# Layer 0 of a two-layer trunk: a new order of the input products, the gates' products ahead of their sigmoids, and one sum of the attention behind a split

## The chip, the cores and the metric

The kernel runs on one core of one Trainium2 chip, in one launch. The metric is device time in microseconds (us), the median of several executions. The engines by the names of the profile: PE multiplies matrices (PEld loads its weights), DVE is VectorE, ACT is ScalarE, POOL is GpSimd, SP issues most DMAs.

## The reference

A trunk of two layers over 256 positions of width 2048, in float32. Layer 0 projects the normed input into six parts of 1024 columns, runs two recurrences on them side by side, and multiplies their joined outputs by `w_out`. Layer 1 is a dilated windowed attention. Each layer ends in a squared-ReLU MLP. The part that the change is about, cut:

```python
def rg_lru(xb, w_a, b_a, w_i, b_i, lam):          # xb: conv of the x part, 4 blocks of 256
    r = sigmoid(xh @ w_a + b_a); i = sigmoid(xh @ w_i + b_i)      # block by block
    log_a = -LRU_C * r * softplus(-lam)
    a = exp(log_a)
    u = sqrt(-expm1(2.0 * log_a)) * (i * xf)
    return associative_scan(lambda l, r: (l[0] * r[0], r[0] * l[1] + r[1]), (a, u), axis=1)[1]

def recurrent_mixers(h, ...):
    x_lru, y_lru, q_h, f_h, v_h, g_h = split(h @ w_in)
    lru = rg_lru(causal_depthwise_conv(x_lru, conv_w, conv_b), ...) * gelu(y_lru)
    hg = hgrn2(q_h, f_h, v_h, g_h, lower_bound, g_norm)   # per head: normed, times silu(g_h)
    return concatenate([lru, hg], axis=-1) @ w_out
```

## The kernel before

**Products.** Every float32 operand is split into a rounded high part and the rest: `hi` is a cast on ACT (L130), `lo` is weight minus `hi` on DVE (L131). A product is three passes on PE: high by high, high by low, low by high (`mm`, L221). The weights come as blocks of 128x2048 in a fixed list of units; `fetch` loads the next block into one of three `raw` buffers and casts it, two units ahead of the one in use. `hi` has three buffers, so the cast of a block waits for the last product that reads the block three units earlier. Activations are split in the same way by `split_to`: a copy on ACT (L267, or L270 with a gain) and a subtraction on DVE (L268, or L271).

**Layer 0's input products.** `tokens_group` computes 512 columns of the projection in four units of 24 products, into two banks `p` of PSUM (three buffers), and ACT copies them out as a tile `tk` (L369). The names are those of the string ORDER: x and y are the input and the gelu branch of the RG-LRU (two groups each), q, f, v and g belong to HGRN2 (two groups each), and G0 and G1 are the block-diagonal gates of the two RG-LRU groups (`lru_gates`): four banks each, alternately `p` and `pl`, and in each bank two products of 256 columns, each with its sigmoid (L252, priority by `urgent`), followed by the gates' tail on ACT and DVE (L623 to L632), which ends in a scan.

**Ticks.** Everything else of layer 0 is cut into generators, in lanes: a and b hold HGRN2's chunks (`hgrn`), c the convolution (`lru_in`), the gelu (`lru_gelu`) and the RG-LRU's output (`lru_out`), d HGRN2's norm and output gate (`finish`). Each group of products has a list in TICKS of up to eight entries; after every twelve products the next entry advances the lanes that it names. `turned` transposes four 128x128 blocks on PE (L224) into a bank with one buffer each: `po` for `lru_in`, `lru_out` and `finish`; `pd` and `pt` for `hgrn`. Whoever writes such a bank waits until its last reader is done.

**Order on each engine.** A scheduler fixes the order of the instructions on every engine when the kernel is built, by its own costs and priorities; at run time each engine takes its queue strictly in that order, as the rows of the trace show. `after(...)` adds a tie that says which of two instructions of one engine comes first.

**Output product and attention.** `out_project` multiplies the two halves of the mixers' output (`bufb`, 16 blocks of 128 columns: the first eight from the RG-LRU, the other eight from HGRN2) by `w_out`, in the order of its last argument. The large products of both layers use sums of weight blocks: `combine` loads blocks, adds them on DVE (L159) or by an accumulating DMA of POOL (L174), and splits the sums like any block.

Of the kernel before, what the change touches and what calls it, by code (L numbers as in the profile page):

```python
# [10 lines left out]
F32 = mybir.dt.float32  # L11
# [4 lines left out]
AF = mybir.ActivationFunctionType  # L16
OP = mybir.AluOpType
# [3 lines left out]
P = 128  # L21
S = 256
# [19 lines left out]
def trunk_kernel(ctx, tc, head, x, xtok, cols, tab, masks, pos, fin, w_in, w_gate, w_out, w_qkv, w_o, w1, w2, out):  # L42
# [3 lines left out]
    act = pool("act")  # L46
# [5 lines left out]
    pmm = pool("pmm", 3, space=PSUM)  # L52
    psc = pool("psc", 1, space=PSUM)

    stream = lambda: tc.high_priority(offset=PRIO)
    urgent = lambda: tc.high_priority(offset=URGENT)
    V, A, T = nc.vector, nc.scalar, nc.tensor
# [18 lines left out]
    bufb = Chunks()  # L76
# [7 lines left out]
    units = []  # L84
    made = {}
# [11 lines left out]
    for g, step in enumerate(ORDER.split()):  # L97
        if step[0] == "G":
            units.append((w_gate, int(step[1])))
        else:  # L100
            units.extend((w_in, 4 * PLACE[step] + i) for i in range(4))
    units.extend((w_out, 4 * n + g) for n in range(2) for g in (0, 2, 1, 3))
    plan2(w_out, 8)
    for layer in range(2):
        if layer:
# [47 lines left out]
    def combine(u, src, i, what, i0):  # L153
        def load(name, j, home=wraw):
            held[name] = home.tile([P, 2048], F32, name="raw" if home is wraw else name)
            nc.sync.dma_start(held[name], src[j])

        def add(to, x, y):
            return V.tensor_tensor(held[to], held[x], held[y], OP.add)  # L159

        if what == "a":
            load("t1", i0 + 4, both)
            load("a", i)
            held["s"] = both.tile([P, 2048], F32, name="s")
            add("s", "a", "t1")
        elif what in ("n", "d"):
            load(what, i)
        def make(step=2048):
            made[u] = Weights(held[{"t1": "s", "t2": "s", "t3": "t1", "t4": "s"}.get(what, what)], step)

        ahead = units[u + 1][2:3] if u + 1 < len(units) else ()
        if ahead == ("t2",):
            load("c", i0 + 5)
            nc.gpsimd.dma_start(held["t1"], src[i0 + 5], accum_op=OP.add)  # L174
            if (src is w2 and i0 == LATE_SUM) or (src is w1 and i0 == 64):
                make()
                after(add("s", "s", "c"), [made[u].ins.name])
                return
            add("s", "s", "c")
        make(2048 if what != "t2" else 0)  # L180
        if what == "t2":
            waiting.append(made[u])
        if what == "c":
            nc.gpsimd.dma_start(held["s"], src[i0 + 1], accum_op=OP.add)
# [66 lines left out]
    def lut(out_, in_, func, **kw):  # L251
        i = A.activation(out_, in_, func, **kw)  # L252
        if luts["kind"] != tables[func]:
            luts.update(kind=tables[func], before=luts["now"], now=[])
        luts["now"].append(after(i, luts["now"][:1] or luts["before"]))

    def direct(p, w, jobs):
        for blk, mov, first, last in jobs:
            h, l = w.part(blk * P, P)
            mm(p, h, mov[:, :S], start=first, stop=False)  # L260
            mm(p, h, mov[:, S:], start=False, stop=False)
            mm(p, l, mov[:, :S], start=False, stop=last)
# [114 lines left out]
    m = tmp.tile([P, 2], F32, name="nm2", bufs=2)  # L377
# [91 lines left out]

    rotary()  # L470
    done = {"v0": vfirst}
    outs, roots = {}, {}

    def turned(name, tiles, at):
        p = psc.tile([P, 2, S], F32, name=name, bufs=1)
        for i, (z, m) in enumerate(zip(tiles, at)):
            for j in range(2):
                turn(p[:, i, j * P:j * P + P], z[:, j, m * P:m * P + P])
        return p
# [90 lines left out]
    def finish(g, half):  # L570
        if not half:
            hs = roots[g]
            V.tensor_scalar(hs, hs, 1.0 / P, EPS, op0=OP.mult, op1=OP.add)
            roots[g] = wk.tile([P, 8], F32, name="hr", bufs=2)
            rsqrt(roots[g], hs, 8)
        pair_ = [2 * half, 2 * half + 1]
        for at in pair_:
            o, z = outs[4 * g + at], done[f"g{g}"][:, :, at * P:at * P + P]
            s = wk.tile([P, 2, P], F32, name="g", bufs=2)
            lut(s, z, AF.Sigmoid)  # L580
            V.tensor_tensor(s, s, z, OP.mult)
            for j in range(2):
                V.scalar_tensor_tensor(o[:, j], o[:, j], roots[g][:, 2 * at + j:2 * at + j + 1], s[:, j],
                                       op0=OP.mult, op1=OP.mult)
        yield
        p = turned("po", [outs[4 * g + at] for at in pair_], (0, 0))
        if g and not half:
            bufb.tiles[3] = act.tile([P, 4, 2 * S], F32R, name="bufb3")
        for i, at in enumerate(pair_):
            split_to(bufb[:, 8 + 4 * g + at], p[:, i], col("gn", 4 * g + at))  # L590
        yield
# [15 lines left out]

    def lru_gates(gp):
        w = unit(w_gate, gp)
        room = act.tile([P, 8, S], F32, name="bufb3")  # L610
        gr, gi = room[:, :4], room[:, 4:]
        for m in range(4):
            b = 4 * gp + m
            both_p = psc.tile([P, 512], F32, name="pl", bufs=2) if m % 2 else pmm.tile([P, 512], F32, name="p")
            for gate, (g, bname) in enumerate(((gr, "b_a"), (gi, "b_i"))):
                p = both_p[:, gate * S:gate * S + S]
                direct(p, w, [(gate * 8 + 2 * m + k, bufb[:, (b // 2) * 2 + k], k == 0, k == 1)
                              for k in range(2)])
                with urgent():
                    lut(g[:, m], p, AF.Sigmoid, bias=col(bname, b))  # L620
        for m in range(4):
            b = 4 * gp + m
            V.tensor_tensor(xc[:, b], xc[:, b], gi[:, m], OP.mult)  # L623
            lut(gi[:, m], gr[:, m], AF.Tanh, scale=sp4[:, b:b + 1])
            lut(gr[:, m], gr[:, m], AF.Exp, scale=sp8[:, b:b + 1])
            V.tensor_scalar(gi[:, m], gi[:, m], -1.0, 1e-30, op0=OP.mult, op1=OP.max)
        for m in range(4):
            b = 4 * gp + m
            lut(gi[:, m], gi[:, m], AF.Sqrt)
            V.scalar_tensor_tensor(gi[:, m], gr[:, m], 1.0, gi[:, m], op0=OP.add, op1=OP.mult)  # L630
            V.tensor_tensor(xc[:, b], xc[:, b], gi[:, m], OP.mult)
            V.tensor_tensor_scan(xc[:, b], gr[:, m], xc[:, b], 0.0, op0=OP.mult, op1=OP.add)  # L632

    def lru_gelu(n):
        y = done[f"y{n}"]
        q = outs[f"y{n}"] = vgs.tile([P, 2, 512], F32, name="tk", bufs=7)
        for j in range(2):
            A.activation(q[:, j], y[:, j], AF.Square, scale=math.sqrt(0.044715))
            V.scalar_tensor_tensor(q[:, j], q[:, j], 1.0, y[:, j], op0=OP.add, op1=OP.mult)
            lut(q[:, j], q[:, j], AF.Sigmoid, scale=2.0 * math.sqrt(2.0 / math.pi))  # L640
            V.tensor_tensor(y[:, j], y[:, j], q[:, j], OP.mult)
            yield

    def lru_out(n, half):
        b0 = 4 * n + 2 * half
        p = turned("po", [done[f"y{n}"]] * 2, (2 * half, 2 * half + 1))
        z = outs[f"y{n}"][:, half].rearrange("p (i s) -> p i s", i=2)
        V.tensor_tensor(z, p, xc[:, b0:b0 + 2], OP.mult)
        split_to(bufb[:, b0:b0 + 2], z)
        yield  # L650

    def reload():
        for j in range(2):
# [2 lines left out]
    lanes.update(a=[hgrn(0), hgrn(2)], b=[hgrn(1), hgrn(3)],  # L656
                 c=[lru_in(0, 0), lru_in(0, 1), lru_in(1, 0), lru_in(1, 1),
                    lru_gelu(0), lru_out(0, 0), lru_out(0, 1), lru_gelu(1), lru_out(1, 0), lru_out(1, 1)],
                 d=[finish(0, 0), finish(0, 1), finish(1, 0), finish(1, 1)])
    for step in ORDER.split()[1:]:  # L660
        if step == "g1":
            reload()
        if step[0] == "G":
            lru_gates(int(step[1]))
        else:
            done[step] = tokens_group(step, rt)
# [8 lines left out]
    def close_mixers():  # L675
# [3 lines left out]
        formx = both.tile([P, 4, 2, 512], F32R, name="formx")  # L679
        pair, formh = open_pairs(0)  # L680

    ticks[:] = TICKS["o0"].split()
    steps[:] = [[], [], [close_mixers]]

# [253 lines left out]
                second(layer * 64 + q * 16, n, ends, r2, r2n, done, gains if ends and not gname and not n else None)  # L938
        return fing

    nrm = out_project(w_out, "nmlp0", (0, 2, 1, 3))
    nx1 = Norm()
    mlp(0, nrm, nx1, "nmix1")
    pairs.close()
# [192 lines left out]
LATE_SUM = 56  # L1137
PRIO = 150
URGENT = 400
ORDER = "v0 q0 f0 x0 q1 f1 v1 x1 G0 g0 y0 G1 y1 g1"  # L1140
TICKS = {
# [11 lines left out]
}  # L1153
PLACE = {step: n for n, step in enumerate(step for step in ORDER.split() if step[0] != "G")}
WARM = 9
# [101 lines left out]
```

## Time and profile before

| | us |
|---|---|
| median of 3 runs | 2153.93 |
| lowest and highest | 2153.9, 2154.84 |
| profiled execution | 2153.29 |
| span in its trace | 2151.5 |
| PE busy | 2127.6 (99%) |
| DVE busy | 1781.4 (83%) |
| ACT busy | 1307.3 (61%) |

The mean granted clock of PE is 0.996. Layer 0's input products lie in the first 330 us of the span, the attention's first products around 1130 us. Rows of the timeline name start, duration, engine, line, operation, written tile, read tiles and shape; what stands in brackets is the idle time of that engine just before, and what ended it. Matmuls are pipelined, and the modelled end of one lies beyond the start of the next.

### The profile page before, as it was taken

To read this page: it belongs to the slowest core of one execution; us is meant where nothing else is said; L and a number is where in the kernel's file an instruction comes from. 1 tells how busy PE (TensorE), PEld (TensorE's weight loads), DVE (VectorE), ACT (ScalarE), POOL (GpSimd) and SP (SyncE) were. 2 spreads that over 40 slices of the span, in tenths; PEclk is the share of its full clock that TensorE was granted. 3 is DMA by queue.
4 is the path that set the end of the run, shared out by engine and by line. 5 is a ranking of instruction groups with operands and counts; after the bars stand their busy time and mean duration, and the time that the engine had idled before them with its cause. 6 is when DMAs were issued, how large, how long until landed. Compare 5 with 4: busy or idle time off the path is not lost.

```text
span 2151.5 us, 24903 instructions
## 1 busy us (share of the span) xinstructions
PE 2127.6 (99%) x9854; PEld 1770.5 (82%) x9854; DVE 1781.4 (83%) x1687; ACT 1307.3 (61%) x1305; POOL 72.3 (3%) x89
## 2 busy tenths in 40 slices
PE   9999889999999999999999999999999999999998
PEld 7888778888888888888887888888888888888887
DVE  7666567988888889889897888698987988888897
ACT  7443665666557557557665666666655755755764
POOL 0000000000000000000000000000000000000000
PEclk9999899999999999999999999999999999999999
DMA  8444445778887877878687766667778788777885
GB/s 340 161 152 141 153 157 205 229 236 248 273 249 229 280 245 238 256 263 247 222 271 250 237 202 213 217 187 258 236 242 273 247 242 259 267 237 245 267 268 156
DMA packets 70164, 500.12 MB, mean 232 GB/s; under 512 B 7840, under 2 KB 8096, under 8 KB 10272
## 3 DMA queue, kind: packets, MB, share of 16 engines
q1 hardware_dynamic: 57888, 412.99, 50.6%
q0 software_dynamic: 11872, 84.94, 21.1%
q8 instruction: 77, 1.26, 0.2%
q10 hardware_dynamic: 288, 0.61, 0.1%
q14 instruction: 39, 0.32, 0.0%
HBM read 496.41 MB, written 2.10 MB: 232 GB/s over the span
## 4 chain that ended last, share of the span: by engine, by line
PE 95%; ACT 2%; DVE 1%; DMA 1%; issue 0%; SPq 0%; DVEq 0%; ACTq 0%
PE p L221 60%; PE pd L221 15%; PE po L221 14%; PE pl L224 2%; PE pt L221 2%; PE pl L221 2%; DVE lo L131 1%; ACT hi L130 1%; DMA raw<-in_w_qkv 0%; ACT bufb L252 0%; DMA both_in<-in_head 0%; PE po L224 0%; ACT L252 0%; ACT bufa L270 0%; DVE bufb L630 0%
## 5 line engine op out<-in xcount | busy, mean ns | idle before, releaser
L130 ACT CAST hi<-raw 128x2048 fp32r<-128x2048 f32 (+1 forms) x364 | 659.3, 1817 | 537.4 <-PE p L221 341.3
L131 DVE TENSOR_TENSOR lo<-raw,hi 128x2048 fp32r<-128x2048 f32 (+1 forms) x364 | 789.0, 2171 | 223.2 <-ACT hi L130 221.6
L221 PE MATMUL p<-hi,bufa 128*128 128x512 f32 x2000 | 650.8, 395 | 0.4 <-ACT bufa L270 0.4
L221 PEld LDWEIGHTS p<-hi,bufa 128*128 128x128 f32 x2000 | 376.8, 188 | 77.8 <-ACT bufa L270 0.7
L221 PE MATMUL p<-hi,bufb 128*128 128x512 f32 x1264 | 405.0, 391 | 0.0
L221 PE MATMUL p<-lo,bufa 128*128 128x512 f32 x1000 | 390.4, 390 | 2.0 <-DVE lo L131 1.8
L131 DVE TENSOR_TENSOR lo<-s,hi 128x2048 fp32r<-128x2048 f32 x120 | 274.2, 2285 | 11.5 <-ACT hi L130 9.4
L221 PEld LDWEIGHTS p<-hi,bufb 128*128 128x128 f32 x1264 | 237.3, 188 | 48.9
L130 ACT CAST hi<-s 128x2048 fp32r<-128x2048 f32 x120 | 229.6, 1913 | 53.8 <-PE po L221 23.1
L221 PE MATMUL p<-lo,bufb 128*128 128x512 f32 x632 | 246.0, 389 | 0.0
L221 PEld LDWEIGHTS p<-lo,bufa 128*128 128x128 f32 x1000 | 188.7, 189 | 40.5 <-DVE lo L131 3.3
L221 PEld LDWEIGHTS p<-lo,bufb 128*128 128x128 f32 x632 | 118.7, 188 | 24.3
L221 PE MATMUL pd<-hi,bufa 128*128 128x512 f32 x352 | 116.7, 393 | 0.0
L221 PE MATMUL p<-hi,formx 128*128 128x512 f32 x352 | 116.3, 391 | 0.0
L131 DVE TENSOR_TENSOR lo<-t,hi 128x2048 fp32r<-128x2048 f32 x40 | 91.5, 2288 | 15.7 <-ACT hi L130 15.7
L221 PE MATMUL po<-hi,bufb 128*128 128x512 f32 (+1 forms) x320 | 102.4, 386 | 0.0
L159 DVE TENSOR_TENSOR s<-s,raw 128x2048 f32<-128x2048 f32 x40 | 91.3, 2283 | 5.2 <-DMA raw<-in_w_qkv 5.2
L221 PE MATMUL p<-hi,formh 128*128 128x512 f32 x288 | 94.5, 389 | 0.0
L159 DVE TENSOR_TENSOR s<-raw,t 128x2048 f32<-128x2048 f32 x40 | 91.4, 2284 | 0.3 <-DMA raw<-in_w_o 0.3
L221 PE MATMUL po<-hi,bufa 128*128 128x512 f32 x256 | 84.8, 392 | 0.0
L130 ACT CAST hi<-t 128x2048 fp32r<-128x2048 f32 x40 | 76.6, 1915 | 11.6 <-PE pd L221 5.9
L221 PE MATMUL pd<-hi,bufb 128*128 128x512 f32 x256 | 83.0, 389 | 0.0
(316 smaller groups left out, 2791.7 us busy)
## 6 DMA issues: line engine op xcount, KB each, us to landing
raw<-in_w SPq DMA_DIRECT2D x224, 1024.0 KB, 6.5
raw<-in_w_in SPq DMA_DIRECT2D x45, 1024.0 KB, 4.8
raw<-in_w_qkv SPq DMA_DIRECT2D x42, 1024.0 KB, 6.8
t<-in_w SPq DMA_DIRECT2D x32, 1024.0 KB, 6.6
t<-in_w POOLq DMA_DIRECT2D x32, 1024.0 KB, 8.8
s<-in_w POOLq DMA_DIRECT2D x32, 1024.0 KB, 9.2
raw<-in_w_out SPq DMA_DIRECT2D x15, 1024.0 KB, 4.8
raw<-in_w_o SPq DMA_DIRECT2D x15, 1024.0 KB, 4.8
```

The source lines that it names most:

```text
L130: casts[:] = [after(A.copy(h, w), [])]
L131: i = V.tensor_tensor(l, w, h.bitcast(F32), OP.subtract)
L159: return V.tensor_tensor(held[to], held[x], held[y], OP.add)
L221: chain[:] = [after(T.matmul(*args, **kw), chain)]
L224: chain[:] = [after(T.transpose(out_, in_, ident), chain)]
```

## The change

ORDER puts both recurrence inputs (x0, x1) right behind v0, and spreads the gates: G0 comes after them, G1 four groups later. TICKS is rewritten for this order: the convolutions run in x1 and f0, the gates' tails in q0 and v1, the output gates (`finish`) at the end of g1 and in y1, the RG-LRU's outputs in y1 and `o0`, the first group of the output product. `lru_gates` now issues all four accumulations of a bank, both gates, ahead of the two sigmoids. Its tail moves to a generator `lru_scan` in a lane of its own, e, in four pieces for each G. `lru_out` uses the banks `pd` and `pt` instead of `po`. The residual's reload goes ahead of y1 instead of g1. The last gelu's two ticks stand behind the loop. `w_out` is taken in the order 2, 3, 0, 1 instead of 0, 2, 1, 3. In `combine`, the sum of the attention's first query block is tied behind the split of the unit before it. The numbers of lines grow by two, from `lru_scan` on by about ten.

```diff
@@ -99,7 +99,7 @@
             units.append((w_gate, int(step[1])))
         else:
             units.extend((w_in, 4 * PLACE[step] + i) for i in range(4))
-    units.extend((w_out, 4 * n + g) for n in range(2) for g in (0, 2, 1, 3))
+    units.extend((w_out, 4 * n + g) for n in range(2) for g in (2, 3, 0, 1))
     plan2(w_out, 8)
     for layer in range(2):
         if layer:
@@ -162,7 +162,9 @@
             load("t1", i0 + 4, both)
             load("a", i)
             held["s"] = both.tile([P, 2048], F32, name="s")
-            add("s", "a", "t1")
+            i = add("s", "a", "t1")
+            if src is w_qkv and i0 == 8:
+                after(i, [made[u - 1].ins.name])
         elif what in ("n", "d"):
             load(what, i)
         def make(step=2048):
@@ -469,7 +471,7 @@
 
     rotary()
     done = {"v0": vfirst}
-    outs, roots = {}, {}
+    outs, roots, rooms = {}, {}, {}
 
     def turned(name, tiles, at):
         p = psc.tile([P, 2, S], F32, name=name, bufs=1)
@@ -607,29 +609,35 @@
 
     def lru_gates(gp):
         w = unit(w_gate, gp)
-        room = act.tile([P, 8, S], F32, name="bufb3")
-        gr, gi = room[:, :4], room[:, 4:]
+        room = rooms[gp] = act.tile([P, 8, S], F32, name="bufb3")
         for m in range(4):
             b = 4 * gp + m
-            both_p = psc.tile([P, 512], F32, name="pl", bufs=2) if m % 2 else pmm.tile([P, 512], F32, name="p")
-            for gate, (g, bname) in enumerate(((gr, "b_a"), (gi, "b_i"))):
-                p = both_p[:, gate * S:gate * S + S]
-                direct(p, w, [(gate * 8 + 2 * m + k, bufb[:, (b // 2) * 2 + k], k == 0, k == 1)
-                              for k in range(2)])
-                with urgent():
-                    lut(g[:, m], p, AF.Sigmoid, bias=col(bname, b))
-        for m in range(4):
-            b = 4 * gp + m
-            V.tensor_tensor(xc[:, b], xc[:, b], gi[:, m], OP.mult)
-            lut(gi[:, m], gr[:, m], AF.Tanh, scale=sp4[:, b:b + 1])
-            lut(gr[:, m], gr[:, m], AF.Exp, scale=sp8[:, b:b + 1])
-            V.tensor_scalar(gi[:, m], gi[:, m], -1.0, 1e-30, op0=OP.mult, op1=OP.max)
-        for m in range(4):
-            b = 4 * gp + m
-            lut(gi[:, m], gi[:, m], AF.Sqrt)
-            V.scalar_tensor_tensor(gi[:, m], gr[:, m], 1.0, gi[:, m], op0=OP.add, op1=OP.mult)
-            V.tensor_tensor(xc[:, b], xc[:, b], gi[:, m], OP.mult)
-            V.tensor_tensor_scan(xc[:, b], gr[:, m], xc[:, b], 0.0, op0=OP.mult, op1=OP.add)
+            p = psc.tile([P, 512], F32, name="pl", bufs=2) if m % 2 else pmm.tile([P, 512], F32, name="p")
+            for gate in range(2):
+                direct(p[:, gate * S:gate * S + S], w,
+                       [(gate * 8 + 2 * m + k, bufb[:, (b // 2) * 2 + k], k == 0, k == 1) for k in range(2)])
+            with urgent():
+                for gate, bname in enumerate(("b_a", "b_i")):
+                    lut(room[:, 4 * gate + m], p[:, gate * S:gate * S + S], AF.Sigmoid, bias=col(bname, b))
+
+    def lru_scan(gp):
+        gr, gi = rooms[gp][:, :4], rooms[gp][:, 4:]
+        for half in range(2):
+            for m in range(2 * half, 2 * half + 2):
+                b = 4 * gp + m
+                V.tensor_tensor(xc[:, b], xc[:, b], gi[:, m], OP.mult)
+                lut(gi[:, m], gr[:, m], AF.Tanh, scale=sp4[:, b:b + 1])
+                lut(gr[:, m], gr[:, m], AF.Exp, scale=sp8[:, b:b + 1])
+                V.tensor_scalar(gi[:, m], gi[:, m], -1.0, 1e-30, op0=OP.mult, op1=OP.max)
+            yield
+        for half in range(2):
+            for m in range(2 * half, 2 * half + 2):
+                b = 4 * gp + m
+                lut(gi[:, m], gi[:, m], AF.Sqrt)
+                V.scalar_tensor_tensor(gi[:, m], gr[:, m], 1.0, gi[:, m], op0=OP.add, op1=OP.mult)
+                V.tensor_tensor(xc[:, b], xc[:, b], gi[:, m], OP.mult)
+                V.tensor_tensor_scan(xc[:, b], gr[:, m], xc[:, b], 0.0, op0=OP.mult, op1=OP.add)
+            yield
 
     def lru_gelu(n):
         y = done[f"y{n}"]
@@ -643,7 +651,7 @@
 
     def lru_out(n, half):
         b0 = 4 * n + 2 * half
-        p = turned("po", [done[f"y{n}"]] * 2, (2 * half, 2 * half + 1))
+        p = turned("pt" if half else "pd", [done[f"y{n}"]] * 2, (2 * half, 2 * half + 1))
         z = outs[f"y{n}"][:, half].rearrange("p (i s) -> p i s", i=2)
         V.tensor_tensor(z, p, xc[:, b0:b0 + 2], OP.mult)
         split_to(bufb[:, b0:b0 + 2], z)
@@ -656,9 +664,10 @@
     lanes.update(a=[hgrn(0), hgrn(2)], b=[hgrn(1), hgrn(3)],
                  c=[lru_in(0, 0), lru_in(0, 1), lru_in(1, 0), lru_in(1, 1),
                     lru_gelu(0), lru_out(0, 0), lru_out(0, 1), lru_gelu(1), lru_out(1, 0), lru_out(1, 1)],
+                 e=[lru_scan(0), lru_scan(1)],
                  d=[finish(0, 0), finish(0, 1), finish(1, 0), finish(1, 1)])
     for step in ORDER.split()[1:]:
-        if step == "g1":
+        if step == "y1":
             reload()
         if step[0] == "G":
             lru_gates(int(step[1]))
@@ -679,6 +688,7 @@
         formx = both.tile([P, 4, 2, 512], F32R, name="formx")
         pair, formh = open_pairs(0)
 
+    tick("cc")
     ticks[:] = TICKS["o0"].split()
     steps[:] = [[], [], [close_mixers]]
 
@@ -938,7 +948,7 @@
                 second(layer * 64 + q * 16, n, ends, r2, r2n, done, gains if ends and not gname and not n else None)
         return fing
 
-    nrm = out_project(w_out, "nmlp0", (0, 2, 1, 3))
+    nrm = out_project(w_out, "nmlp0", (2, 3, 0, 1))
     nx1 = Norm()
     mlp(0, nrm, nx1, "nmix1")
     pairs.close()
@@ -1137,19 +1147,19 @@
 LATE_SUM = 56
 PRIO = 150
 URGENT = 400
-ORDER = "v0 q0 f0 x0 q1 f1 v1 x1 G0 g0 y0 G1 y1 g1"
+ORDER = "v0 x0 x1 G0 q0 f0 q1 f1 G1 v1 g0 y0 g1 y1"
 TICKS = {
-    "f0": ". . . . . a b .",
-    "x0": "a b a b a b a b",
+    "x1": "c c c c c c . .",
+    "q0": ". e . e . e . e",
+    "f0": "c c c c c ac b .",
     "q1": "a b a b a b a b",
-    "f1": "ac bc ac bc ac bc a b",
-    "v1": "a b a b a b a b",
-    "x1": "a b a b a b a b",
-    "g0": "ac bc ac bc ac bc . .",
-    "y0": "d d d d . . . .",
-    "y1": "c . c . c . c .",
-    "g1": ". c c . c . c .",
-    "o0": "d d d d . . . .",
+    "f1": "a b a b a b a b",
+    "v1": "a be a be a be a be",
+    "g0": "a b a b a b a b",
+    "y0": "a b a b a b a b",
+    "g1": "a b a b a b d d",
+    "y1": "dc dc d d dc dc . .",
+    "o0": ". . c c . . . .",
 }
 PLACE = {step: n for n, step in enumerate(step for step in ORDER.split() if step[0] != "G")}
 WARM = 9
```

## The prediction

> **What bounds the kernel now.** I read the page first: the share of each engine and the chain that ended last.
>
> ```profile
> span 2151.5 us, 24903 instructions
> PE 2127.6 (99%) x9854; PEld 1770.5 (82%) x9854; DVE 1781.4 (83%) x1687; ACT 1307.3 (61%) x1305; POOL 72.3 (3%) x89
> PE 95%; ACT 2%; DVE 1%; DMA 1%; issue 0%; SPq 0%; DVEq 0%; ACTq 0%
> ```
>
> PE sets the time. The change leaves PE the same products, so it can only win or lose where PE stands still or runs slowly. The waits of PE come second (total, times, longest):
>
> ```profile
> PE p L221 <- ACT bufb L252: 5.2, 4, 2.2
> PE po L224 <- DVE xc L602: 3.2, 1, 3.2
> PE pl L221 <- ACT bufb L252: 2.3, 4, 0.6
> PE p L221 <- DVE lo L131: 1.8, 1, 1.8
> PE po L224 <- DVE tk L641: 1.2, 2, 0.9
> ...
> PE po L224 <- DVE ho L583: 0.5, 1, 0.5
> ```
>
> L252 under `bufb` is the gates' sigmoid, L602 the convolution, L641 the gelu, L583 the HGRN2 output gate. All but `lo` L131 lie in layer 0's input products, and the change touches every one. A wait begins only when the last product's modelled end is over, so I price each place from start to start. The pace comes from the chain, third (start, us, what):
>
> ```profile
> 271.19 5.47 PE p L221 x24
> 292.08 0.73 PE pl L221 x6
> ```
>
> A 512-wide product costs 5.47/24 = 0.228 us, a 256-wide one 0.73/6 = 0.12. Fourth, windows over G0, G1 and stretches of 3.4 us (start:end, us, then busy time and count of PE, PEld, DVE, ACT, POOL; granted clock; DMA):
>
> ```profile
> 216.80:230.50 13.70, 10.13 (x52) 9.10 (x52) 4.26 (x5) 5.67 (x11) 0.00 (x0) 0.66 0.26 92
> 287.90:298.60 10.70, 6.78 (x50) 5.93 (x49) 4.08 (x5) 6.21 (x10) 0.00 (x0) 1.00 0.54 196
> 217.87:221.29 3.42, 1.57 (x12) 1.50 (x12) 2.33 (x2) 2.23 (x5) 0.00 (x0) 0.99 0.00 0
> 221.29:224.70 3.41, 2.85 (x14) 2.63 (x12) 0.81 (x2) 0.95 (x2) 0.00 (x0) 0.50 0.76 247
> 231.53:234.94 3.41, 3.41 (x9) 2.64 (x9) 2.48 (x2) 3.39 (x6) 0.00 (x0) 0.51 0.01 2
> 245.18:248.59 3.41, 1.56 (x9) 1.18 (x8) 3.41 (x6) 2.17 (x2) 0.00 (x0) 1.00 0.96 341
> 1150.70:1154.10 3.40, 1.82 (x9) 1.17 (x7) 3.40 (x2) 1.92 (x2) 0.00 (x0) 1.00 0.01 5
> ```
>
> Each G step has 48 256-wide products, 5.8 us at pace, but G0 took 13.7 and G1 10.7. In G0 the clock also halved, from 221.3 to 234.9, past the gates' end.
>
> **The change part by part.**
>
> *Both products ahead of both sigmoids.* Before, the second gate's products write the bank that the first gate's sigmoid is still reading, so every bank holds one wait; there are eight, the 4+4 rows above. Now no product waits within its own bank, and with both recurrence inputs computed early the two G steps meet inputs that are long ready. G1 loses 10.7-5.8 = 4.9 us. G0 loses 13.7-5.8 = 7.9, and ten 512-wide products after it that ran at half clock lose 10 x 0.2 = 2.0:
>
> ```profile
> 230.66 4.77 PE p L221 x12
> 219.72 0.51 PE L221 MATMUL p<-bufb,hi 128*128 128x256 f32 x2 [1.88 <-ACT bufb L252]
> L252 ACT ACTIVATE bufb<-p,c__91 128x256 f32<-128x256 f32 x8 | 3.8, 474 | 5.5 <-PE p L221 5.5
> ```
>
> (4.77/12 = 0.40 against 0.228.) Gates together 14.8. The sigmoids now run behind the products: a bank's two are 0.95 us of ACT against 12 products, 1.4 us of PE, and the four banks of a G are different ones, so a product waits only for a bank's reader from before G. If that cover failed, one `hi` cast ahead of the reader would show as 1.9 us, as in the second row.
>
> *Convolution (L602), gelu (L641), output gate (L583).* These transposes waited for VectorE's queue:
>
> ```profile
> 249.98 0.63 PE L224 MATMUL po<-tab__183,tk 128*128 128x128 f32 x4 [3.24 <-DVE xc L602]
> 313.41 0.30 PE L224 MATMUL po<-tab__183,tk 128*128 128x128 f32 x1 [0.94 <-DVE tk L641]
> 270.17 1.02 PE po L224 x4
> 276.66 0.57 PE po L224 x4
> ```
>
> At 249.98 VectorE had the first gates' tail (L623 to L632) between two convolutions. The tail now has fixed ticks in q0 and v1, where no transposes of a convolution stand. 3.3 us go; the gelu's 0.94 and 0.21 with their slow transposes 1.5; L583's 0.5 and the 1.02 us that four transposes took in place of 0.57, together 0.95.
>
> *Attention's first query sum.* Rows of the timeline (with the instruction's shape) and of the chain:
>
> ```profile
> 1134.93 2.29 DVE L159 TENSOR_TENSOR s<-raw,t 128x2048 f32<-128x2048 f32 x1
> 1133.35 1.91 ACT L130 CAST hi<-raw 128x2048 fp32r<-128x2048 f32 x1
> 1137.14 2.30 DVE lo L131
> 1139.45 10.26 DMA raw<-in_w_qkv
> 1149.80 0.09 DVE s L159
> 1152.01 2.30 DVE lo L131
> 1154.35 5.51 PE p L221 x23
> 1152.14 0.39 PE L221 MATMUL p<-hi,bufa 128*128 128x512 f32 x1
> ```
>
> The product after 1152.14 was due at 1152.37 and began at 1154.35: 1.98 lost. The first `lo` freed the raw buffer that the 10.26 us load waited for, and stood behind the sum though its cast was done at 1135.26. Putting the sum behind it lets `lo`, load, sum and the second `lo` come 1.88 earlier: 0.1 is left. Queued behind the sum now: POOL's accumulating load into `t`, 2.6 us later (the sum ends at 1139.8, not at 1137.2); its data are not needed until after the sum of 1149.80. The saving is bounded by 0 (the earlier load shares the DMA engines longer) and 1.98; I take 1.9.
>
> Removed: 14.8 + 3.3 + 1.5 + 0.95 + 1.9 = 22.4 us.
>
> *What it adds: y1's second tick.* `finish` writes its transposes to the one bank `po`, and the next `finish` needs that bank read by both L271 (L273 after). The new order puts `finish` at g1's last ticks and at "dc dc" of y1. Before, in y0:
>
> ```profile
> 274.54 0.47 DVE L271 SCALAR_TENSOR_TENSOR bufb<-po,c__91,bufb 128x256 fp32r<-128x256 f32 x1
> 275.98 0.47 DVE L271 SCALAR_TENSOR_TENSOR bufb<-po,c__91,bufb 128x256 fp32r<-128x256 f32 x1
> 276.60 0.63 PE L224 MATMUL po<-tab__183,ho 128*128 128x128 f32 x4
> ```
>
> The second L271 ended at 276.45 and the transposes began at 276.60, with nothing to spare. In the order built for the change, one more pair of casts stands ahead of that second L271: on ACT the `hi` cast of the third weight block ahead is queued before the second L270, on VectorE its `lo` before the second L271. This `hi` takes over the buffer that the last product ahead of the transposes reads. So the transposes wait from that product through the whole pair:
>
> ```profile
> L130 ACT CAST hi<-raw 128x2048 fp32r<-128x2048 f32 x19 | 36.1, 1901 | 27.5 <-PE p L221 24.9 <-PE pl L221 2.5
> L131 DVE TENSOR_TENSOR lo<-raw,hi 128x2048 fp32r<-128x2048 f32 x19 | 43.5, 2289 | 23.7 <-ACT hi L130 23.6
> L271 DVE SCALAR_TENSOR_TENSOR bufb<-po,c__91,bufb 128x256 fp32r<-128x256 f32 x6 | 2.9, 478 | 0.5 <-ACT bufb L270 0.5
> ```
>
> 0.39 (a product, start to end) + 1.90 + 2.29 + 0.48 + 0.15 (handover, 276.45 to 276.60) = 5.2, less the 0.23 that the product takes anyway: 5.0 us, within 4.5 and 5.5. Later ticks of y1 have the same distance, but the stall has put ACT and VectorE 5 us ahead of PE, so they wait for nothing.
>
> *Clock.* During those 5 us PE is idle for 4.8. The waits over 1.8 us were 1.88 (G0), 3.24, 2.2 (G1) and 1.8 (at 1152); the clock fell after the first alone, and came back after one window of 3.41 us that PE filled. An idle of 4.8 is longer than all of them, so I take a fall, for one window: 3.41 us at half clock is 1.7 lost. Bounds 0 and two windows, 3.4. The Trainium skill ("TensorE: Matmul & The Clock Gate", Part 1) says that the clock halves after a wholly idle window of about 3.4 us and returns after a busy one; an estimate by that page is a fall in (4.8-3.41)/3.41 = 4 of 10 phases, which would make the sum 1.7 lower in the other six. This trace disagrees with its first half: the fall at 221.3 followed a window with 1.57 us of work, and the same 1.56 at 245.18 brought none.
>
> *Convolutions' banks.* Under L602 stands:
>
> ```profile
> L602 DVE SCALAR_TENSOR_TENSOR xc<-po,c__91,xc 128x255 f32<-128x255 f32 x4 | 1.9, 481 | 0.1
> ```
>
> In x1 and in f0 two convolutions follow each other in `po` with one weight's casts and three L602 (0.48 each) between: 0.39 + 1.90 + 2.29 + 1.44 + 0.15 = 6.2 against 25 products, 5.7. I take 0.4 for each, 0.8 together; bounds 0 and 1.2.
>
> *Moved at no cost.* `lru_out` in `pd` and `pt`, which HGRN2 uses in other ticks; the reload ahead of y1, its loads queued on SP between weight loads; w_out in order 2, 3, 0, 1, so that the HGRN2 half, ready first, leads; the last gelu behind the loop, whose `lru_out` follows at o0's third tick, 36 products or 8.2 us later. The products hide them all; with that cover gone, each costs about what the gelu's wait did, 1.5.
>
> Sum: 2153.29 (profiled execution; its span is 2151.5) - 22.4 + 5.0 + 1.7 + 0.8 = 2138.4. The median before is 0.6 above the profiled run, so the median after is 2139.0.
>
> **The rivals.**
> - *No new wait.* If the casts are done in time in y1, only the 0.8 stays: 2132.3. For it: y0's handover cost nothing. Against: the built order. Chance 0.15.
> - *Wait without fall of the clock* gives 2137.3, two windows 2140.7; both belong to my forecast, own range 2135 to 2143, chance 0.63.
> - *Other waits move in.* The 1.9 at 1152 stays because the load takes longer, or one covered move fails (1.5), or a G step meets a cast (1.9): one to three of these give 2141 to 2145. Against: in the list of waits nothing of layer 0 stands outside the places removed. Chance 0.12.
> - *On the other side: `po` as a lock.* If each of the seven handovers of `po` (four convolutions and four `finish` follow each other in it) waits for a pair of casts, it costs 7 x 5.0 = 35 and the kernel gets 35 - 22.4 + 1.7 = 14.3 slower: 2168. It decides from the sixth on (30 + 1.7 against 22.4 + 4.3). For it: one wait of 3.24 at L602 before. Against: two `finish` in y0 changed over without a wait, and in the built order only y1's second tick has the pair of casts between with no room. Chance 0.05.
> - *It doesn't do what it says.* If two banks of each G still wait for a reader behind a 1.9 cast, that is 4 x 1.9 = 7.6, and with G0's fall of the clock (13.7 - 5.8 - 5.0 + 2.0 = 4.9, by G1's 5.0 of waits) 12.5: 2151.5. For it: ACT's queue holds a cast at each weight block. Against: the built order puts the sigmoids behind all products of their bank, and four banks. Chance 0.05.
>
> **How the numbers follow.** About 0.2% (4.3 us) can be told from no change. Forecast 0.63, no new wait 0.15, others 0.12, the lock 0.05, not doing what it says 0.05. Faster holds the first three: 0.90; same 0.05; slower 0.05. Two in ten may be left out: the range goes from 2 us below the no-wait case, 2130.3 (seven terms removed, each read to about 0.3 us), to 1 us above the upper end of the third case, 2146. The predicted time is 2139.0.
>
> **What would show it.** PE's waits have no row with L252 under `bufb`, none with L602 above 0.7 and none with `lo` L131 above 0.3; each G step spans under 6.5 us at clock 1.0; one row `po` from L273 of 4 to 5 us in y1, a window of clock 0.5 behind it. Wrong would be a wait over 1 us at any other place in layer 0's input products, or a step of layer 1 other than this sum that changes.

## The result and the profile after

The changed kernel takes 2137.9 us (median of 4 runs, 2137.32 to 2138.93) against 2154.39 us before (4 runs, 2153.9 to 2155.35): ratio 0.9923, 95% interval 0.9906 to 0.9941. The forecast was 2139.0. The profiled execution took 2137.32 us with a span of 2135.5, 16.0 less than before. The page after, and its chain by engine:

```profile
span 2135.5 us, 24906 instructions
PE 2119.7 (99%) x9854; PEld 1766.3 (83%) x9854; DVE 1780.0 (83%) x1687; ACT 1308.2 (61%) x1307; POOL 72.3 (3%) x89
PE 99%; DVE 1%; ACT 0%; DMA 0%; issue 0%
```

The chain is now PE for 99% of the span, 95% before. The waits of PE (total, times, longest):

```profile
PE po L226 <- DVE bufb L273: 4.8, 1, 4.8
PE po L283 <- DVE e L411: 1.1, 1, 1.1
PE p L223 <- ACT bufa L272: 1.0, 1, 1.0
PE po L226 <- DVE xc L604: 0.8, 2, 0.4
```

The rows of the gates' sigmoid, of the gelu, of the output gate and of the split in the attention are gone. What is new is one wait of 4.8 us on L273; the wait on the convolution is down from 3.2 to two of 0.4. L411 and L272 belong to the opening. The two G steps, in windows:

```profile
73.38:79.13 5.75, 5.75 (x49) 5.75 (x48) 2.78 (x3) 5.52 (x8) 0.00 (x0) 1.00 0.49 181
182.49:188.32 5.83, 5.83 (x50) 5.83 (x50) 4.02 (x5) 4.79 (x10) 0.00 (x0) 1.00 0.19 53
```

5.75 and 5.83 us, PE busy throughout, at full clock, in place of 13.7 and 10.7. The chain through y1:

```profile
301.87 5.47 PE p L223 x24
...
307.37 1.91 ACT hi L130
...
309.30 2.29 DVE lo L131
...
311.59 0.41 DVE bufb L273
312.00 0.14 issue
312.13 1.09 PE po L226 x4
313.22 6.34 PE p L223 x24
319.56 0.44 PE po L226 x4
```

This is the new wait, link by link: the last product of a unit, the cast of the block that takes over its buffer, the subtraction, then L273, and only then the transposes. Behind it four transposes take 1.09 us in place of 0.44, and 24 products 6.34 in place of 5.47: 1.5 us lost to a half clock. In the attention the chain no longer leaves PE:

```profile
1130.18 2.72 PE pt L223 x12
1132.90 2.72 PE pd L223 x12
1135.62 6.57 PE p L223 x29
```

### The profile page after: what moved, and what is told of

It is laid out like the page before. It is cut to its first block, busy times and chain, and to the rows that moved or that the text cites. A ratio compares the mean times of both kernels' runs of the same rounds, so it can differ in the third digit from the quotient of the medians.

```text
span 2135.5 us, 24906 instructions
## 1 busy us (share of the span) xinstructions
PE 2119.7 (99%) x9854; PEld 1766.3 (83%) x9854; DVE 1780.0 (83%) x1687; ACT 1308.2 (61%) x1307; POOL 72.3 (3%) x89
## 4 chain that ended last, share of the span: by engine, by line
PE 99%; DVE 1%; ACT 0%; DMA 0%; issue 0%
PE p L223 62%; PE pd L223 15%; PE po L223 14%; PE pt L223 3%; PE pl L226 2%; PE pl L223 2%; DVE lo L131 0%; ACT hi L130 0%; PE po L226 0%; DMA both_in<-in_head 0%; DVE xc L604 0%; PE pd L226 0%; PE pt L226 0%; ACT xall L1137 0%; ACT z L302 0%
```

## The experiments

Times are medians; "before" is the kernel before on the same chip. Where less than a microsecond matters I go by the rows of the traces, since medians of one kernel on one chip spread over 1 to 3 us. The 2137.9 of the changed kernel was measured in a set of its own; the kernel before lies at 2153.5 to 2154.7 in the four sets, so a difference from 2137.9 is good to about 1 us.

Traces differ in the opening as well: the 101st matmul of PE starts at 25.1 us in the changed kernel and at 26.5 in the first run below, where products of 512 columns start 0.43 us apart until 9.4 us into the span, against 0.23 there from 7.2 us on. "Behind the opening" means that I compare the starts of the same matmuls of PE from the 101st on.

**The bank of y1's wait.**

```diff
-        p = turned("po", [outs[4 * g + at] for at in pair_], (0, 0))
+        p = turned("pd" if half and not g else "po", [outs[4 * g + at] for at in pair_], (0, 0))
```

> The changed kernel with one edit: the second finish of y1 writes its transposes to the bank pd instead of po. My theory (the 4.8 us wait in y1 is the bank po, held by a subtraction that stands behind a pair of casts, and the fall of the clock follows from the idle time): the wait on L273 is gone, no window at clock 0.5 stands behind it, and the kernel is 5.0 + 1.4 = 6.4 us faster than the changed one, about 2131.5 us. Rival (the casts themselves are late, whatever the bank): the wait of about 5 us moves to the next weights or transposes of y1 and the time stays at 2137.9. Rival on the clock (it falls by where the 3.4 us windows lie, not by the wait): the wait goes, a half-clock window stays, 2133.

Measured: 2131.67 us (2131.38 to 2132.16), ratio to before 0.9896 (0.9882 to 0.9911), 6.2 below the changed kernel. The chain of this kernel in y1:

```profile
302.75 0.44 PE po L226 x4
303.19 5.46 PE p L223 x24
308.65 0.44 PE pd L226 x4
309.09 5.46 PE p L223 x24
314.55 0.44 PE po L226 x4
```

PE passes all three transposes without a stop, at full clock. Behind the opening the two traces differ by 6.5 us, the 4.96 of the wait from start to start and the 1.5 of the half clock. So the bank held the wait, and the half-clock window came from the wait. Both rivals fall.

**Spacing f0.** With that edit, the second convolution of f0 one tick later.

```diff
-    "f0": "c c c c c ac b .",
+    "f0": "c c c . c ac bc .",
```

> The edit of the bank as in the run before, and in f0 the second convolution one tick later. My theory: of the two waits on L604 (0.4 idle, 0.57 from start to start each) the one in f0 goes, the one in x1 stays, and nothing new comes: about 2130.9 us. Rival (the convolution delayed pushes HGRN2's first chunk behind it): a new wait of 0.5 or more in q1, 2131.5 or above.

Measured: 2131.61 us (2130.21 to 2131.95). PE's waits on the convolution in this kernel:

```profile
PE po L226 <- DVE xc L604: 0.4, 1, 0.4
```

One of two is left, the one in x1, and no wait came in q1. The median's 0.06 us is within the spread and shows nothing; the row does, and behind the opening this trace is 0.59 us shorter than that of the run before.

**Both banks.** The second convolution of x1 also goes to `pd`.

```diff
-        p = turned("po", [done[f"x{n}"]] * 2, (2 * half, 2 * half + 1))
+        p = turned("pd" if half and not n else "po", [done[f"x{n}"]] * 2, (2 * half, 2 * half + 1))
```

> The changed kernel with the second finish of y1 and the second convolution of x1 in pd, and in f0 the second convolution one tick later. My theory: no wait of PE is left in layer 0's products behind the opening; 0.57 us less than with the wait in x1 alone: 2131.0 us, clock 1.0 from the opening to the last microseconds. Rival (a convolution in pd keeps HGRN2's first chunk from that bank): a wait of 0.5 or more in f0 or q1.

Measured: 2130.11 us (2129.96 to 2131.3), ratio 0.9886 (0.9869 to 0.9902): the fastest version, 7.8 us below the changed kernel. A window over nearly the whole of it:

```profile
100.00:2115.00 2015.00, 2015.00 (x9367) 1679.00 (x9366) 1702.60 (x1525) 1233.51 (x1201) 71.53 (x84) 1.00 0.74 234
```

PE is busy 2015.00 of 2015.00 us at clock 1.00: in this stretch the profile shows no wait that is left to remove. Behind the opening the trace is 7.6 us shorter than the changed kernel's, 6.5 for y1 and 1.1 for the two convolutions.

**The sum of the attention.** Taken out of the changed kernel, put alone into the kernel before, and taken out of the kernel with both banks. The edit each time, away or in:

```diff
-            i = add("s", "a", "t1")
-            if src is w_qkv and i0 == 8:
-                after(i, [made[u - 1].ins.name])
+            add("s", "a", "t1")
```

> The changed kernel without the tie of the attention's first query sum. My theory: the wait of PE for lo of L131 at the attention's third unit is back with 1.8 us (1.98 from start to start), everything ahead of it is as in the changed kernel, and the time is 2137.9 + 1.9 = 2139.8 us. Rival (the new order of layer 0 shifts the loads so that the wait is gone anyway): no wait there, 2137.9. The same 4.8 us wait stands in y1: if its idle time alone makes the clock fall, a half-clock window follows here too; if the place of the windows matters, it may not, and the time is 1.4 lower.

> The kernel before with only the tie of the attention's first query sum. My theory: PE's wait for lo of L131 (1.8) is gone, all other waits stay, 2154.4 - 1.9 = 2152.5 us. Rival (the load starts 1.9 us earlier but shares the DMA engines and lands as late): the wait stays above 1 us and the time within 0.5 us of 2154.4.

> The run before without the tie of the attention's first query sum. In a kernel with no other wait the tie's worth stands by itself. My theory: the load of the third raw block takes 8.8 to 10.3 us as in the traces so far, so PE's wait for lo of L131 is 0.4 to 1.9 us, and the time 0.5 to 2.0 above the run before, 1.7 more if that wait brings a half-clock window: 2131.5 to 2134.7. Rival (the tie is worth nothing without the old order of layer 0): no wait, the time of the run before.

Without the tie the changed kernel took 2139.32 us (2138.53 to 2141.63), the kernel with both banks 2132.76 (2130.63 to 2133.53). In the first of them the 4.8 us wait in y1 was followed by one half-clock window, as in the changed kernel. The split's wait in these two traces, in that order:

```profile
PE p L221 <- DVE lo L131: 0.4, 1, 0.4
```

```profile
PE p L221 <- DVE lo L131: 1.9, 1, 1.9
```

The load behind it differed, again in that order:

```profile
1126.09 8.83 DMA raw<-in_w_qkv
```

```profile
1118.12 10.35 DMA raw<-in_w_qkv
```

The wait is 1.5 us longer because the load took 1.5 longer (10.26 in the trace before). So the tie is worth 0.4 to 1.9 us of waiting with the load, not a steady 1.8 as I expected; from a matmul ahead of the sum to one behind it the two traces lose 0.7 and 2.2 us. In the nine traces with the tie the largest wait on `lo` here is 0.2; in the four without it (before and the gates alone are the other two) it is 0.4 to 1.9. The differences of the medians, 1.4 and 2.7, are of that size but within a few tenths to two microseconds of spread.

Alone in the kernel before it gave 2153.18 against 2153.52 us, ratio 0.9998 (0.9989 to 1.0007): not resolved. Its trace tells why the 1.9 doesn't show there:

```profile
PE po L226 <- DVE xc L604: 5.2, 1, 5.2
PE p L223 <- DVE lo L131: 0.2, 1, 0.2
```

The split's wait is down to 0.2, so the rival, a load that lands as late, falls: the trace gains 2.1 us at the sum. But the convolution's wait is 5.2 in place of 3.2, and the edit does not touch it: up to the sum every engine runs the same instructions in the same order in both traces. In this execution the granted clock was 1.0 through G0 and fell only behind that wait and in G1:

```profile
242.98:246.39 3.41, 0.00 (x0) 0.00 (x0) 3.38 (x8) 0.63 (x2) 0.00 (x0) 1.00 0.53 161
287.35:290.76 3.41, 1.33 (x11) 1.33 (x12) 1.73 (x1) 2.86 (x4) 0.00 (x0) 1.00 0.64 267
290.76:294.17 3.41, 2.84 (x14) 2.55 (x13) 1.60 (x4) 1.11 (x3) 0.00 (x0) 0.50 0.52 156
```

The rows of both traces show the link. PE starts the four products ahead of these transposes at 241.24 us, 4.9 earlier than before (246.14), but VectorE starts the convolution's last two operations only 3.0 earlier (245.89, before 248.87), so the wait is 1.9 longer. A half clock in G0 and the wait behind it partly replace each other in the kernel before, and which of them comes changes from execution to execution. Layer 0 is 1.7 us longer here behind the opening, and that hides most of the 2.1.

**The gates alone.** Only the gates' products ahead of the sigmoids, in the kernel before.

```diff
-            for gate, (g, bname) in enumerate(((gr, "b_a"), (gi, "b_i"))):
-                p = both_p[:, gate * S:gate * S + S]
-                direct(p, w, [...])
-                with urgent():
-                    lut(g[:, m], p, AF.Sigmoid, bias=col(bname, b))
+            for gate in range(2):
+                direct(p[:, gate * S:gate * S + S], w, [...])
+            with urgent():
+                for gate, bname in enumerate(("b_a", "b_i")):
+                    lut(room[:, 4 * gate + m], p[:, gate * S:gate * S + S], AF.Sigmoid, bias=col(bname, b))
```

> The kernel before with only the gates' products of a bank ahead of its two sigmoids; order, ticks, tail and banks stay. My theory: the eight waits on the gates' sigmoid go and the clock stays up, 14.8 us, but the tail, now 5 to 9 us early against PE, stands in front of the same convolution and the same output gates: the wait on L602 grows from 3.2 to about 5.6, that on L583 from 0.5 to about 4, so that about 8 us remain: 2146 us (2143 to 2149). Rival (each part is worth its own term of the sum): 2154.4 - 14.8 = 2139.6 us.

Measured: 2144.17 us (2142.72 to 2146.12), ratio 0.9957 (0.9941 to 0.9974), 10.0 below the 2154.16 of before. PE's waits in it:

```profile
PE po L224 <- DVE xc L602: 5.0, 1, 5.0
PE p L221 <- DVE lo L131: 1.9, 1, 1.9
...
PE po L224 <- DVE tk L641: 1.0, 2, 0.8
...
PE po L224 <- DVE ho L583: 0.5, 1, 0.5
```

No wait on a sigmoid is left, but the convolution's has grown by 1.8 and brought two half-clock windows of its own; a third came in the attention, behind the 1.9 on `lo`. So the rival, 14.8, falls: alone, the gates' term is worth 10.0, and part of its gain turns into the next wait. My 4 us at the output gate did not come; it stayed at 0.5.

**The old gates in the new order.** The reverse of that diff, in the changed kernel.

> The changed kernel with the gates' products and sigmoids of a bank in turn, as before. My theory: four waits on the sigmoid come back in each G, the first 3.7 (a copy out of the last tokens, a cast and a table load stand ahead of it) in G0 and 2.0 in G1, then about 0.6 each: 5.5 + 3.8 = 9.3 us, and about 2 more if the clock falls: 2147 to 2149.5 us. Rival (the new places alone hide the sigmoids): waits under 1 us in all, 2138 to 2139.

Measured: 2156.26 us (2154.64 to 2160.99), ratio 1.0015 (1.0006 to 1.0025): slower than before. The waits are those that I expected:

```profile
PE p L223 <- ACT bufb L254: 6.6, 4, 3.6
...
PE pl L223 <- ACT bufb L254: 2.3, 4, 0.6
```

What I missed is the clock. The windows of this kernel from the first of them on:

```profile
74.46:77.87 3.41, 1.06 (x8) 0.81 (x6) 0.52 (x1) 3.01 (x3) 0.00 (x0) 1.00 0.79 305
77.87:81.29 3.42, 2.13 (x10) 2.13 (x11) 1.77 (x1) 1.67 (x3) 0.00 (x0) 0.50 0.26 41
81.29:84.70 3.41, 2.85 (x13) 2.55 (x13) 0.43 (x1) 0.86 (x3) 0.00 (x0) 0.50 0.66 274
84.70:88.11 3.41, 2.85 (x14) 2.55 (x13) 0.42 (x1) 0.86 (x3) 0.00 (x0) 0.50 0.00 0
88.11:91.53 3.42, 2.86 (x13) 2.46 (x13) 0.43 (x1) 1.09 (x3) 0.00 (x0) 0.50 0.00 0
91.53:94.94 3.41, 3.41 (x10) 2.64 (x9) 1.90 (x1) 3.39 (x6) 0.00 (x0) 0.50 0.00 0
```

Five windows at 0.5, 17.1 us: the later waits fall into windows that are followed by another at 0.5, and half of the 17.1, about 8.5, comes on top of the 9 us of waits. By the medians 18.4 us are lost in all, behind the opening of the two traces 17.3. Three of the ten executions took 2160 to 2161 us at a mean granted clock of 0.990 to 0.991, against 0.994 in the others, so the time at half clock changes between executions. With the old gates, the new order gains nothing over the kernel before.

**`lru_out` in `po` again.**

```diff
-        p = turned("pt" if half else "pd", [done[f"y{n}"]] * 2, (2 * half, 2 * half + 1))
+        p = turned("po", [done[f"y{n}"]] * 2, (2 * half, 2 * half + 1))
```

> The changed kernel with lru_out in the bank po again. My theory: in y1 and o0 lru_out and finish then follow each other in po at neighbouring ticks and wait for each other's reader behind casts, 2 to 6 us more in all: 2140 to 2144 us. Rival (the 4.8 us wait in y1 has put the other engines far enough ahead): nothing over 0.5 us, 2137.9.

Measured: 2147.22 us (2146.8 to 2149.82), ratio 0.997 (0.9958 to 0.9981). The row of L273 grows to three waits:

```profile
PE po L226 <- DVE bufb L273: 11.3, 3, 4.8
```

6.5 us of waits beside the one of the changed kernel, and half-clock windows of 10.2 us in place of 3.4. The waits lie where the theory put them, their sum is a little over its range, and the rival falls; with the clock the kernel is 9.3 slower than the changed one.

**w_out in the old order.**

```diff
-    nrm = out_project(w_out, "nmlp0", (2, 3, 0, 1))
+    nrm = out_project(w_out, "nmlp0", (0, 2, 1, 3))
```

(and the units in the same order)

> The changed kernel with w_out in the order 0, 2, 1, 3 again. My theory: the RG-LRU's second half, finished last, is now read by the third unit in place of the fourth, and PE waits there for its split, 3.4 us, on L270 (the split's subtraction): about 2141.3 us. Rival (hidden behind the products): 2137.9.

Measured: 2143.28 us (2142.48 to 2143.79), ratio 0.9952 (0.9937 to 0.9967). New waits of PE:

```profile
PE p L223 <- DVE bufb L270: 2.0, 1, 2.0
...
PE p L223 <- ACT bufb L269: 0.8, 1, 0.8
```

2.8 idle (3.1 from start to start) and one more half-clock window: 5.4 against the changed kernel, where I expected 3.4 of waiting and no fall.

**The tails at once.** The gates' tails behind their G, not at the ticks of lane e.

```diff
+        for _ in lru_scan(gp):
+            pass
...
-                 e=[lru_scan(0), lru_scan(1)],
+                 e=[],
```

> The changed kernel with the gates' tails right behind their G in place of the ticks in q0 and v1. My theory: the order of the groups removed the wait on the convolution, not the fixed places of the tail; no new wait over 0.3 us comes and the time stays at 2137.9 (within 1). Rival (the fixed places carry it): the tail of G0 stands on VectorE in front of the convolutions of f0 or the tail of G1 in front of HGRN2's pieces, a wait of 2 to 3 us comes back there, 2140 to 2141 us. On the clock: the 4.8 us wait in y1 stays, and by the eight waits of 4.8 us and more seen so far, all followed by a fall, a half-clock window follows here too.

Measured: 2138.89 us (2137.51 to 2139.13). PE's waits in layer 0's products are those of the changed kernel, 4.8 and two of 0.4. The clock was down for two windows behind the 4.8, not one; behind the opening the trace is 1.4 us longer than the changed kernel's, and that comes at these windows. G0's tail lies where it lay: its scans run at 93.36 to 95.80 us, with the ticks at 93.14 to 95.57. Only G1's moved, its last scans from 225.96 to 204.75. So the fixed places carry no wait of PE in this order.

## Why the prediction was right

- **Gates, 14.8 us.** Right in size: G0 and G1 lie at 5.75 and 5.83 us against the 5.8 of the pace, and no half clock follows. The mechanism, a wait of the second gate's products for the first gate's sigmoid, is shown from both sides, by the gates alone and by the old gates in the new order.
- **Convolution, gelu, output gate, 5.75 us.** The waits went as priced. The reason that I gave for the first, the tail's fixed ticks in q0 and v1, was wrong: with the tail at once nothing comes back. What took the tail away is the order. Before, the convolutions of x1 ran in g0, right behind G0, and VectorE had them among the tail's scans (L632); now they run in f0, with all of q0 between (L639 is the scan, L604 the convolution). Rows of VectorE before, then after:

```profile
247.31 0.46 DVE L602 SCALAR_TENSOR_TENSOR xc<-po,c__91,xc 128x253 f32<-128x253 f32 x1
247.68 1.26 DVE L632 TENSOR_TENSOR_SCAN xc<-bufb,xc 128x256 f32<-128x256 f32 x2
```

```profile
93.14 2.43 DVE L639 TENSOR_TENSOR_SCAN xc<-bufb,xc 128x256 f32<-128x256 f32 x4
105.84 1.51 DVE L604 SCALAR_TENSOR_TENSOR xc<-po,c__91,xc 128x253 f32<-128x253 f32 x3
```

The tail ends 10 us ahead of the first of them. With the gates alone, in the old order, the wait stayed. Why the gelu's and the output gate's waits went was not tested apart.
- **Attention's sum, 1.9 us.** In the changed kernel's trace the wait is gone, and PE gains 2.1 us there on the trace before. The size was read from one execution; without the tie the wait was 0.4 to 1.9, by the time of the load.
- **y1's second tick, 5.0 us.** 4.80 idle, 4.96 from start to start, in the order cast, subtraction, L273, transposes, as worked out. The reason that I gave for the later ticks of y1, a stall that puts ACT and VectorE ahead, does not hold: with the bank `pd` there is no stall, and none of them waits.
- **Clock, one window, 1.7 us.** One window of 3.41 us came, at 1.5 us. The reason was weak: I argued from an idle longer than others. That it had to come follows from the figures of the last section. The estimate from the Trainium skill ("TensorE: Matmul & The Clock Gate", Part 1), four phases of ten, does not fit these traces: a fall followed each of their eight waits of 4.8 us and more, and one of 4.65 (the eight that I counted ahead of the run with the tails at once were seven and the 4.65).
- **Convolutions' banks, 0.8 us.** Two of 0.4 idle, 0.57 from start to start, 1.14 in all.
- **Moved at no cost.** So in the changed kernel: none of these places has a row among its waits. The runs with `po` and with the old order of w_out show that these two moves were needed: 9.3 and 5.4 us. The reload and the last gelu were not tested apart.

The terms gave 14.9 us less for the profiled execution, its span shows 16.0. Of the 1.1 between them 0.3 lies in the opening, which the change doesn't touch, and 0.2 at the attention's sum; the other 0.6 lies in layer 0's products, and I don't assign it to a term.

## What to carry to other kernels

Where one engine sets the time, add up its waits from start to start and read the order of the queues that they hang on; a fix in one place only shows if the next wait on the same path goes too (gates alone 10.0 of 14.8). In this kernel a bank with one copy needs its reader's last instruction ahead of the next long cast in both queues, or another bank: moving one set of transposes to a bank that was free at that tick won 6.2 us here by the medians, 6.5 by the traces. Price a wait of PE above 1.9 us with the half clock that can follow it, above all where more waits stand behind it.

## What the runs showed of the hardware

I had not expected how sharply the clock goes by stretches of 3.41 us. Within a trace the falls and returns lie on one grid of 3.413 us, and its phase differs between executions. On that grid, rows of the kernel before:

```profile
217.84:221.25 3.41, 1.53 (x13) 1.50 (x12) 2.29 (x1) 2.27 (x5) 0.00 (x0) 1.00 0.00 0
245.15:248.56 3.41, 1.59 (x10) 1.21 (x8) 3.41 (x6) 2.17 (x2) 0.00 (x0) 1.00 0.95 339
```

The first was followed by a fall, the second was not. The changed kernel, and the kernel with the gates alone in its attention:

```profile
308.17:311.58 3.41, 0.00 (x0) 0.00 (x0) 3.11 (x6) 2.08 (x4) 0.00 (x0) 1.00 0.62 259
311.58:315.00 3.42, 2.87 (x9) 2.51 (x10) 2.81 (x10) 0.95 (x2) 0.00 (x0) 0.50 0.65 218
```

```profile
1141.49:1144.90 3.41, 1.53 (x7) 1.10 (x7) 3.41 (x3) 3.41 (x2) 0.00 (x0) 1.00 0.04 10
```

In all thirteen traces, between the opening and the last microseconds, each of the 14 falls followed a stretch in which PE was busy 1.53 us or less, and no stretch with 1.59 or more was followed by one. By these figures a fall needs some 1.9 us of idle in one stretch (3.41 - 1.53 = 1.88). An idle time under that can't bring one by itself; one of 3.8 or more, split over two stretches at worst, always must (3.8/2 = 1.9); between them the phase decides, as with the 3.24 us of the kernel before, which brought none, and the first 3.6 with the old gates, which did. The Trainium skill ("TensorE: Matmul & The Clock Gate", Part 1) names an idle window as the condition; these rows show falls after windows with 45% of work (1.53 of 3.41 us). For the return, half-clock stretches with up to 2.51 us of work were followed by another, as in the old gates' rows, and those with 3.11 to 3.41 us by the full clock. From 2.79 to 2.87 us both occur: the changed kernel returned after 2.87, the old gates stayed down after 2.85 and 2.86. Busy time rests on modelled ends, so where that bound lies stays open.
